# Two exponentials issued behind an output eviction, FFT butterflies behind mixing sums, and an input split into quarters

## The chip, the cores and the metric

The kernel runs on one core of a Trainium2 chip. The metric is the device time of one execution in microseconds (us). Three executions of the kernel before gave 787.26, 787.35 and 787.60 us, and their median, 787.35 us, is the time before.

The core has a matrix engine (TensorE, here PE), a vector engine (DVE), a scalar or activation engine (ACT), a general engine (GpSimd, here POOL) and a queue that issues most transfers (SyncE, here SP). Each engine works through its own list of instructions in order and waits at an instruction until what that instruction reads is there and what it overwrites is done with. SBUF is the on-chip memory, PSUM the accumulators that PE writes.

## What is computed

One encoder layer on x of 2048 rows by 1024 columns, in float32: a projection of all rows, two token mixers, an output projection and a norm.

```python
proj = jnp.einsum('bsd,de->bse', x, w_in[l])
q, k, v, gf_lr, gb_lr, z_gla, u, z_fnet = jnp.split(proj, _OFFSETS, axis=-1)
...
log_af = jax.nn.log_sigmoid(gf_lr @ w_gate_up_fwd + b_gate_fwd) / GATE_TAU
o = _gla_chunked(q, k, v, log_af) + flip(_gla_chunked(flip(q), flip(k), flip(v), flip(log_ab)))
y_gla = rms_norm(o) * gla_norm_g * jax.nn.silu(z_gla)
...
uf = jnp.fft.fft2(ug, axes=(1, 3), norm='ortho').real
y_fnet = einsum(uf, w_fnet) * jax.nn.silu(z_fnet)
...
x = _layernorm(DEEPNORM_ALPHA * x + concatenate([y_gla, y_fnet]) @ w_out, ln_g, ln_b)
```

(The lines are condensed.) The first mixer is a gated linear attention in both directions, four heads; the second is a Fourier transform over the 2048 positions and over the 128 columns of each of four groups.

## The kernel before, in words

Products keep float32 accuracy: `split` (L52) writes an operand as a rounded high part (a cast on ACT, L55) and a low part (a subtraction on DVE, L58), and each product is three matmuls: high by high, high by low, low by high. The rows are taken in eight blocks of 256. There are four stages, one after the other on PE.

**First stage (to about 262 us).** The projections for the two output gates and for u.

**Second stage (262 to 398 us), `phase2`.** Two generators take turns in a loop (L738): `qk_all` (L708), the projections to q and k, and `fnet_pe` (L675), the Fourier branch. `qk_block` (L608) is 96 matmuls of one block at L86, in four runs of 24, and yields after each run. Its x comes through `load_x` (L71): two halves of 128x1024, each a load into `xraw` (two buffers) and one split into `xhl` (four buffers), made at the start of the block before. For each group of 128 columns, `fft(g)` (L515) does the butterflies of a 16-point transform on DVE (L522, L523, L534, L531; `fw` is the array that they work on) and splits the result into four tiles `bhl`. `stage2` (L620) multiplies these with a table (L635) and splits the product into `yhl`; `mixdown` (L640) multiplies that with the group's map (L655) into two PSUM tiles, one of which ACT copies to `qs`, and DVE writes their sum and difference to `yf` (L661, L662). While PE works through the five sets `ks` of one group, DVE also does the butterflies of the next one, a piece at each `next(nf)` (L693, L700). `gate_f` (L665) then multiplies `yf` with the gate on POOL. `et` and `wcs` are the tables, split in the same way.

**Third stage (398 to about 580 us), `phase3`.** The attention, in a loop over b (L963) in which three blocks overlap. PE projects block b to gate inputs and v (`pw_part`, `pv_part`, L94), transposes the gate inputs `rn` (L813; ACT copies the result to `R`, L814) and multiplies them up to gates (L825). For block b-1 it makes scores (L905, L906), and for b-1 and b-2 state updates (L928) and outputs (L935) in `gla_b`. ACT copies a state update to `S` (L930, L932) and the output to `oi` (L939). DVE sums the gates (two scans, L843 and L845), subtracts the value in the chunk's middle (L866) and clips (L867). `gates3` (L869) then takes two exponentials on ACT (L872 into `c`, L873 into `g`), two products on DVE (L891 into `qp`, L892 into `g`), and `alphas`: four small sums on DVE into `tf` and two small exponentials (L952, L953). `chain_f` (L1199) carries the state from chunk to chunk on POOL: an addition (L1194), which needs `S`, and a product with `alpha` (L1197). `gate_evac` (L779) takes a gate input tile from PSUM: two casts on ACT (L781, L782) and a subtraction on DVE (L783), once for each half of the block's rows.

**Fourth stage (to the end), `phase4`.** Output projection (L1220), residual and norm.

The order on each engine is chosen by a scheduler from the order in which the program is written and its estimates of durations. `issue_after(x)` is an extra rule for it: what is written inside comes behind x in the list of x's own engine. It adds no wait. Inside `gates3` it takes hold where x runs on the same engine.

Of the kernel before, what the change touches and what calls it, by code (L numbers as in the profile page):

```python
# [43 lines left out]
class Kern:  # L44
# [454 lines left out]
    def phase2(self):  # L499
        nc, a = self.nc, self.a  # L500
        with ExitStack() as ctx:
# [138 lines left out]
            def mixdown(g, ks, yhl, yv):  # L640
# [11 lines left out]
                for i in (1, 0):  # L652
                    pp = self.pg([P, 2, P])
                    for j, (s, mv) in enumerate(((0, 0), (0, 1), (1, 0))):
# [4 lines left out]
                nc.scalar.copy(out=qs[:, 0:n], in_=pq[0][:, 0:n])  # L659
                k0 = ks[0]  # L660
                nc.vector.tensor_tensor(out=yv[:, k0:k0 + n, :], in0=pq[1][:, 0:n], in1=qs[:, 0:n], op=ALU.add)  # L661
                nc.vector.tensor_tensor(out=yv[:, 16 - k0:16 - k0 - n:-1, ::-1], in0=pq[1][:, 0:n],  # L662
                                        in1=qs[:, 0:n], op=ALU.subtract)

            def gate_f(g, yf):  # L665
                for b in range(NBLK):
                    zf = yps[1].tile([P, BLK], F32, name="zfl", tag="zfl", bufs=4)
                    nc.sync.dma_start(out=zf, in_=self.zf_d[b][:, g, :])
                    yb = yf[:, b * BLK:(b + 1) * BLK]
                    (nc.gpsimd if g < 3 else nc.vector).tensor_tensor(out=yb, in0=yb, in1=zf, op=ALU.mult)  # L670
                    if b % 2:
                        bs = slice((b - 1) * BLK, (b + 1) * BLK)
                        nc.sync.dma_start(out=self.mf_d[:, g, bs], in_=yf[:, bs])

            def fnet_pe():  # L675
                bt = bt0
# [8 lines left out]
                for g in range(4):  # L685
# [4 lines left out]
                    for ks in ((1, 2), (3, 4), (5, 6), (7,), (0, 8)):  # L690
                        with self.tc.issue_after(self.qk_mm.ins):
                            yhl = stage2(g, bt, ks)
                        next(nf, None)  # L693
                        yield
                        if pend:
                            pend()
                        pend = lambda a=(g, ks, yhl, yv): mixdown(*a)
                        if ks[0] == 0:
                            pend = lambda a=(g, ks, yhl, yv), yf=yf: (mixdown(*a), gate_f(a[0], yf))
                        next(nf, None)  # L700
                        yield
# [6 lines left out]
            def qk_all():  # L708
                xn = self.x0
                for b in range(NBLK):  # L710
                    xh = xn
                    if b + 1 < NBLK:
                        xn = self.load_x(b + 1)
                    yield from qk_block(b, xh)

            ga, gb = qk_all(), fnet_pe()
            def wvg_load():
# [33 lines left out]
    def phase3(self):  # L751
# [16 lines left out]
        with ExitStack() as ctx:  # L768
# [194 lines left out]
            for b in range(NBLK):  # L963
# [12 lines left out]
                if b > 1:  # L976
                    with after(self.ks_ev, self.at_ev):
                        gates2(b - 1, prev)
                        gates3(b - 1, prev)
                if b > 2:  # L980
                    self.chain_f(2 * b - 3, 2 * b - 1)
                qk_load(b, blk)
# [413 lines left out]
```

## Time and profile before

| | |
|---|---|
| median of three executions | 787.35 us |
| the profiled execution | 788.25 us |
| its span from first to last instruction | 786.5 us |
| mean granted clock of PE, of full speed | 0.995 |
| busy: PE, DVE, ACT, POOL | 748.6, 549.8, 381.1, 196.5 us |
| PE busy from 262 to 398 us (136 us) | 131.23 us |
| PE busy from 398 to 580 us (182 us) | 169.55 us |

A busy time is the sum over an engine's instructions. A row of the timeline gives start, duration, engine, line of the kernel, operation, tile written and tiles read, and in brackets how long the engine stood idle before it and which instruction ended that. Rows of equal instructions that follow each other are joined (x16). The view of waits adds up such idle times by what ended them.

### The profile page before, as it was taken

To read this page: it belongs to the slowest core of one execution; us is meant where nothing else is said; L and a number is where in the kernel's file an instruction comes from. 1 tells how busy PE (TensorE), PEld (TensorE's weight loads), DVE (VectorE), ACT (ScalarE), POOL (GpSimd) and SP (SyncE) were. 2 spreads that over 40 slices of the span, in tenths; PEclk is the share of its full clock that TensorE was granted. 3 is DMA by queue.
4 is the path that set the end of the run, shared out by engine and by line. 5 is a ranking of instruction groups with operands and counts; after the bars stand their busy time and mean duration, and the time that the engine had idled before them with its cause. 6 is when DMAs were issued, how large, how long until landed. Compare 5 with 4: busy or idle time off the path is not lost.

```text
span 786.5 us, 13529 instructions
## 1 busy us (share of the span) xinstructions
PE 748.6 (95%) x5254; PEld 691.2 (88%) x5254; DVE 549.8 (70%) x808; ACT 381.1 (48%) x707; POOL 196.5 (25%) x137
## 2 busy tenths in 40 slices
PE   6999999999999998989999989999998999999995
PEld 5988899999999998989999888889876788888884
DVE  4693467464545789895748888888868777776764
ACT  6674372233223453445546777776655334334341
POOL 0000003020211000213310414444454454544531
PEclk9999999999999999999999999999999999999998
DMA  8876352444126974555775664555455454444222
GB/s 244 267 210 186 118 192 72 150 114 140 68 94 179 272 239 164 156 168 190 239 214 163 185 184 156 154 166 158 139 175 219 168 184 165 166 144 172 108 81 85
DMA packets 81935, 130.75 MB, mean 166 GB/s; under 512 B 7523, under 2 KB 55651, under 8 KB 81862
## 3 DMA queue, kind: packets, MB, share of 16 engines
q1 hardware_dynamic: 79558, 125.60, 50.5%
q10 hardware_dynamic: 2304, 4.20, 1.5%
q8 instruction: 43, 0.70, 0.4%
q14 instruction: 30, 0.25, 0.1%
HBM read 93.07 MB, written 36.70 MB: 165 GB/s over the span
## 4 chain that ended last, share of the span: by engine, by line
PE 55%; DVE 21%; ACT 11%; DMA 8%; issue 3%; SPq 1%; POOL 0%; DVEq 0%; ACTq 0%
PE mm L1220 17%; PE mm L374 17%; PE mm L86 4%; DMA xraw<-in_xt_dram 3%; DVE c L845 3%; PE mm L291 3%; PE mm L94 2%; DVE c L843 2%; ACT xhl L55 2%; DVE fw L534 2%; PE pa L635 2%; DMA fw<-u_d 2%; DVE fw L531 1%; PE pg L291 1%; PE pa L291 1%
## 5 line engine op out<-in xcount | busy, mean ns | idle before, releaser
L94 PE MATMUL mm<-wA_w,xhl 128*128 128x272 f32 x768 | 105.1, 292 | 0.0
L94 PEld LDWEIGHTS mm<-wA_w,xhl 128*128 128x128 f32 x768 | 98.6, 189 | 0.0
L86 PE MATMUL mm<-xhl,wC_w 128*128 128x256 f32 x768 | 96.0, 284 | 0.0
L86 PEld LDWEIGHTS mm<-xhl,wC_w 128*128 128x128 f32 x768 | 93.7, 192 | 0.5 <-issue 0.5
L1220 PE MATMUL mm<-wA_w,mix 128*128 128x512 f32 (+1 forms) x384 | 90.0, 384 | 1.5 <-ACT mix L55 1.1
L1220 PE MATMUL mm<-wB_w,mix 128*128 128x512 f32 (+1 forms) x384 | 89.3, 387 | 0.0
L1220 PEld LDWEIGHTS mm<-wA_w,mix 128*128 128x128 f32 x384 | 70.3, 188 | 16.6 <-ACT mix L55 1.5
L1194 POOL TENSOR_TENSOR S<-S 64x512 f32<-64x512 f32 x30 | 51.2, 1708 | 124.2 <-ACT S L930 121.2
L1220 PEld LDWEIGHTS mm<-wB_w,mix 128*128 128x128 f32 x384 | 69.5, 189 | 13.0
L58 DVE TENSOR_TENSOR xhl<-xraw,xhl 128x1024 fp32r<-128x1024 f32 (+1 forms) x52 | 57.5, 1111 | 29.8 <-ACT xhl L55 29.5
L55 ACT CAST xhl<-xraw 128x1024 fp32r<-128x1024 f32 (+1 forms) x52 | 49.3, 951 | 39.3 <-DMA xraw<-in_xt_dram 20.0
L55 ACT CAST x<-xraw 128x1024 fp32r<-128x1024 f32 x28 | 29.3, 1048 | 69.0 <-PE mm L374 54.9
L436 POOL TENSOR_TENSOR t<-t,t 128x512 f32<-128x512 f32 x7 | 10.9, 1557 | 190.4 <-ACT t L435 190.4
L1318 POOL TENSOR_TENSOR r<-r,lnb 128x1024 f32<-128x1024 f32 x15 | 35.7, 2383 | 89.5 <-issue 51.2
L58 DVE TENSOR_TENSOR x<-xraw,x 128x1024 fp32r<-128x1024 f32 x28 | 37.8, 1352 | 28.7 <-ACT x L55 28.7
L670 POOL TENSOR_TENSOR yf<-yf,zfl 128x256 f32<-128x256 f32 x24 | 20.9, 900 | 121.3 <-ACT yf L649 111.9
L1197 POOL TENSOR_TENSOR S<-S,alpha 64x512 f32<-64x512 f32 x30 | 48.6, 1620 | 2.4
L374 PE MATMUL mm<-wC_s,x 128*128 128x256 f32 x384 | 48.2, 283 | 0.0
L374 PEld LDWEIGHTS mm<-wC_s,x 128*128 128x128 f32 x384 | 47.1, 192 | 0.1
L291 PE MATMUL mm<-xhl,wA_w 128*128 128x512 f32 x192 | 43.9, 389 | 0.0
L291 PEld LDWEIGHTS mm<-xhl,wA_w 128*128 128x128 f32 x192 | 36.0, 188 | 7.4
L55 ACT CAST mix<-zg 128x512 fp32r<-128x512 f32 x15 | 9.3, 622 | 58.8 <-POOL zg L1289 56.0
(210 smaller groups left out, 1497.3 us busy)
## 6 DMA issues: line engine op xcount, KB each, us to landing
xraw<-in_xt_dram SPq DMA_DIRECT2D x48, 512.0 KB, 4.7
xr<-in_x_dram SPq DMA_DIRECT2D x16, 512.0 KB, 3.6
out_dram<-r SPq DMA_DIRECT2D x15, 512.0 KB, 2.7
xraw<-in_xt_dram SPq DMA_DIRECT2D x24, 256.0 KB, 4.7
zg_d<-zs SPq DMA_DIRECT2D x32, 128.0 KB, 3.7
u_d<-t SPq DMA_DIRECT2D x16, 256.0 KB, 3.2
zf_d<-t SPq DMA_DIRECT2D x16, 256.0 KB, 2.4
zfl<-zf_d SPq DMA_DIRECT2D x32, 128.0 KB, 3.4
```

The costliest lines, as they stand in the source:

```text
L55: nc.scalar.copy(out=hi, in_=src)
L58: return (lo_eng or nc.vector).tensor_tensor(out=lo, in0=src, in1=f32(hi), op=ALU.subtract)
L86: mm = self.nc.tensor.matmul(ps, w[:, s, k, c0:c0 + P], x[:, m, k % 4, :], start=(k == 0 and i == 0), stop=(k == KB - 1 and i == 2))
L94: self.nc.tensor.matmul(ps, x[:, s, k % 4, t * P:(t + 1) * P], w[:, m, k, c0:c0 + cols], start=(k == 0 and i == 0), stop=(k == KB - 1 and ...
L291: nc.tensor.matmul(ps[c], self.wzg[:, s, 2 * q + kk, c * P:(c + 1) * P], x[:, m, kk], start=(q == 0 and kk == 0 and j == 0), stop=(q == 3 ...
L374: nc.tensor.matmul(ps[:, i], s_[s][:, k, i * P:(i + 1) * P], m_[m][:, k], start=(k == 0 and j == 0), stop=(k == 3 and j == 2))
L670: (nc.gpsimd if g < 3 else nc.vector).tensor_tensor(out=yb, in0=yb, in1=zf, op=ALU.mult)
L845: V.tensor_tensor_scan(out=c2[64:128, ::-1], data0=r2[64:128, ::-1], data1=g2[64:128, ::-1], initial=0.0, op0=ALU.mult, op1=ALU.add)
L1194: E.tensor_tensor(out=S[ds, dst], in0=S[ds, dst], in1=S[ds, src], op=ALU.add)
L1197: E.tensor_tensor(out=d3, in0=d3, in1=al, op=ALU.mult)
L1220: nc.tensor.matmul(y, c["mix"][:, s, eb], w[:, v, eb % 4, lo:lo + m], start=(ebs[0] == 4 and i == 0), stop=(ebs[0] == 0 and i == len(seq) ...
L1318: nc.gpsimd.tensor_tensor(out=r, in0=r, in1=lnb, op=ALU.add)
```

## The change

Three edits. The two exponentials of `gates3`, from b=2 on, are also to come behind the last copy into `oi` (L939) on ACT. The first butterfly piece of each set of `ks` is to come behind the last difference into `yf` (L662) on DVE. And x for blocks 1 to 7 of the q and k projections is split in quarters: both halves are still loaded at the start of the block before, but a quarter (128x512) is split after each of that block's four yields.

```diff
--- before.py
+++ after.py
@@ -659,7 +659,7 @@
                 nc.scalar.copy(out=qs[:, 0:n], in_=pq[0][:, 0:n])
                 k0 = ks[0]
                 nc.vector.tensor_tensor(out=yv[:, k0:k0 + n, :], in0=pq[1][:, 0:n], in1=qs[:, 0:n], op=ALU.add)
-                nc.vector.tensor_tensor(out=yv[:, 16 - k0:16 - k0 - n:-1, ::-1], in0=pq[1][:, 0:n],
+                self.mix_ev = nc.vector.tensor_tensor(out=yv[:, 16 - k0:16 - k0 - n:-1, ::-1], in0=pq[1][:, 0:n],
                                         in1=qs[:, 0:n], op=ALU.subtract)
 
             def gate_f(g, yf):
@@ -671,6 +671,8 @@
                     if b % 2:
                         bs = slice((b - 1) * BLK, (b + 1) * BLK)
                         nc.sync.dma_start(out=self.mf_d[:, g, bs], in_=yf[:, bs])
+
+            self.mix_ev = None
 
             def fnet_pe():
                 bt = bt0
@@ -690,7 +692,11 @@
                     for ks in ((1, 2), (3, 4), (5, 6), (7,), (0, 8)):
                         with self.tc.issue_after(self.qk_mm.ins):
                             yhl = stage2(g, bt, ks)
-                        next(nf, None)
+                        if self.mix_ev is None:
+                            next(nf, None)
+                        else:
+                            with self.tc.issue_after(self.mix_ev.ins):
+                                next(nf, None)
                         yield
                         if pend:
                             pend()
@@ -708,10 +714,19 @@
             def qk_all():
                 xn = self.x0
                 for b in range(NBLK):
-                    xh = xn
-                    if b + 1 < NBLK:
-                        xn = self.load_x(b + 1)
-                    yield from qk_block(b, xh)
+                    xh, xn, raws = xn, [], []
+                    for hf in range(2 if b + 1 < NBLK else 0):
+                        raw = self.xpool.tile([P, 4, BLK], F32, name="xraw", tag="xraw", bufs=2)
+                        nc.sync.dma_start(out=raw, in_=a["xt"][b + 1, :, 4 * hf:4 * hf + 4, :])
+                        raws.append(raw)
+                    for i, _ in enumerate(qk_block(b, xh)):
+                        yield
+                        if raws and i < 4:
+                            if i % 2 == 0:
+                                t = self.xpool.tile([P, 2, 4, BLK], F32R, name="xhl", tag="xhl", bufs=4)
+                                xn.append(t)
+                            t, js = xn[-1], slice(i % 2 * 2, i % 2 * 2 + 2)
+                            self.split(t[:, 0, js], t[:, 1, js], raws[i // 2][:, js])
 
             ga, gb = qk_all(), fnet_pe()
             def wvg_load():
@@ -976,7 +991,8 @@
                 if b > 1:
                     with after(self.ks_ev, self.at_ev):
                         gates2(b - 1, prev)
-                        gates3(b - 1, prev)
+                        with after(self.oi_ev):
+                            gates3(b - 1, prev)
                 if b > 2:
                     self.chain_f(2 * b - 3, 2 * b - 1)
                 qk_load(b, blk)
```

The lists of PE and POOL are the same as before. Those of ACT and DVE each have 14 splits of 128x1024 replaced by 28 of 128x512. Three places in the lists follow. In the changed kernel line numbers are higher: by 15 in most of `phase2`'s end and `phase3`.

ACT, one turn of the third stage (b=4), before: from the first exponential (L872) to the second half's gate input (`rn`):

```order
L872 ACTIVATE c<-g 128x1024
L781 CAST rn<-mm 128x32
L782 CAST rn<-mm 128x32
L873 ACTIVATE g<-g 128x1024
L930 COPY S<-pg 64x512
L797 COPY v<-mm 128x240
L932 COPY S<-pg 64x512
L939 COPY oi<-pg 128x512
L952 ACTIVATE alpha<-tf 64x8
L953 ACTIVATE alpha<-tf 64x8
L781 CAST rn<-mm 128x32
L782 CAST rn<-mm 128x32
```

and with the change (L887 and L888 are the exponentials, L945 and L947 the copies into `S`, L954 the one into `oi`, L967 and L968 those into `alpha`):

```order
L796 CAST rn<-mm 128x32
L797 CAST rn<-mm 128x32
L812 COPY v<-mm 128x240
L945 COPY S<-pg 64x512
L947 COPY S<-pg 64x512
L954 COPY oi<-pg 128x512
L887 ACTIVATE c<-g 128x1024
L967 ACTIVATE alpha<-tf 64x8
L968 ACTIVATE alpha<-tf 64x8
L888 ACTIVATE g<-g 128x1024
L796 CAST rn<-mm 128x32
L797 CAST rn<-mm 128x32
```

Both exponentials now stand behind the three copies, and the first half's gate input and v ahead of them.

DVE, the start of the second stage, before: x of qk block 1 is the `xhl` row of 128x1024 here and one further ahead:

```order
L534 TENSOR_TENSOR fw<-fw 128x384
L58 TENSOR_TENSOR xhl<-xraw,xhl 128x1024
L534 TENSOR_TENSOR fw<-fw 128x384
L531 SCALAR_TENSOR_TENSOR fw<-fw 128x128 x16
L58 TENSOR_TENSOR et<-eraw,et 128x384
L58 TENSOR_TENSOR bhl<-fw,bhl 128x512 x4
L58 TENSOR_TENSOR et<-eraw,et 128x384
L58 TENSOR_TENSOR xhl<-xraw,xhl 128x1024
```

and with the change:

```order
L531 SCALAR_TENSOR_TENSOR fw<-fw 128x128 x8
L58 TENSOR_TENSOR xhl<-xraw,xhl 128x512
L531 SCALAR_TENSOR_TENSOR fw<-fw 128x128 x8
L58 TENSOR_TENSOR xhl<-xraw,xhl 128x512
L58 TENSOR_TENSOR bhl<-fw,bhl 128x512 x4
L58 TENSOR_TENSOR xhl<-xraw,xhl 128x512
```

The second half of block 1's x was split ahead of the last 16 products and of `bhl`; now two quarters stand among and behind these products, and the last quarter behind all four `bhl`.

DVE, the second stage's group 0, before (L531 are butterflies of the group after next):

```order
L58 TENSOR_TENSOR yhl<-pa,yhl 128x512
L58 TENSOR_TENSOR bhl<-fw,bhl 128x512
L531 SCALAR_TENSOR_TENSOR fw<-fw 128x128 x9
L661 TENSOR_TENSOR yf<-pg,qs 128x2x128
L662 TENSOR_TENSOR yf<-pg,qs 128x2x128
L531 SCALAR_TENSOR_TENSOR fw<-fw 128x128 x6
L58 TENSOR_TENSOR bhl<-fw,bhl 128x512
```

and with the change:

```order
L58 TENSOR_TENSOR yhl<-pa,yhl 128x512
L58 TENSOR_TENSOR bhl<-fw,bhl 128x512
L661 TENSOR_TENSOR yf<-pg,qs 128x2x128
L662 TENSOR_TENSOR yf<-pg,qs 128x2x128
L58 TENSOR_TENSOR bhl<-fw,bhl 128x512
L58 TENSOR_TENSOR yhl<-pa,yhl 128x512
```

The butterflies between the rows of this group's sums are gone; they follow after the group's fourth set.

## Rows read from the trace of the kernel before

**Rows 1.** The page, part 1: busy us, share of the span, instructions
```profile
PE 748.6 (95%) x5254; PEld 691.2 (88%) x5254; DVE 549.8 (70%) x808; ACT 381.1 (48%) x707; POOL 196.5 (25%) x137
```

**Rows 2.** The view of waits, PE: us in total, times, longest us
```profile
PE mm L813 <- DVE rn L783: 5.1, 6, 1.0
PE pg L655 <- DVE yf L662: 4.0, 4, 1.6
PE mm L825 <- ACT R L814: 2.7, 5, 0.8
```

**Rows 3.** Timeline, PE, second stage: start us, us, line, tiles, [idle before <-releaser]
```profile
307.16 0.86 PE L655 MATMUL pg<-yhl,wcs 128*128 128x256 f32 x5 [0.78 <-DVE yhl L58]
...
314.26 0.62 PE L655 MATMUL pg<-yhl,wcs 128*128 128x256 f32 x3 [1.56 <-DVE yf L662]
...
391.46 0.55 PE L655 MATMUL pg<-yhl,wcs 128*128 128x128 f32 x3 [0.30 <-DVE yf L662]
```

**Rows 4.** Timeline, DVE, ahead of the stall at 314.26
```profile
311.37 1.91 DVE L531 SCALAR_TENSOR_TENSOR fw<-fw 128x128 f32<-128x128 f32 x9
...
313.61 0.59 DVE L662 TENSOR_TENSOR yf<-pg,qs 128x256 f32<-128x256 f32 x1
```

**Rows 5.** Timeline, PE, the first two qk blocks
```profile
262.50 16.76 PE L86 MATMUL mm<-xhl,wC_w 128*128 128x256 f32 x135
```

**Rows 6.** Timeline, DVE, while these blocks run
```profile
271.58 1.23 DVE L58 TENSOR_TENSOR xhl<-xraw,xhl 128x1024 fp32r<-128x1024 f32 x1 [0.93 <-ACT xhl L55]
...
273.19 3.32 DVE L531 SCALAR_TENSOR_TENSOR fw<-fw 128x128 f32<-128x128 f32 x16
276.42 0.56 DVE L58 TENSOR_TENSOR et<-eraw,et 128x384 fp32r<-128x384 f32 x1
276.88 2.50 DVE L58 TENSOR_TENSOR bhl<-fw,bhl 128x512 fp32r<-128x512 f32 x4
```

**Rows 7.** Timeline, PE, third stage, one turn of the loop (b=4)
```profile
466.08 0.73 PE L825 MATMUL mm<-R,wg 98*128 98x256 f32 x4 [0.50 <-ACT R L814]
...
478.72 1.06 PE L935 MATMUL pg<-at,v 128*128 128x128 f32 x8
479.53 4.75 PE L94 MATMUL mm<-wA_w,xhl 128*128 128x272 f32 x36
...
485.36 0.32 PE L813 MATMUL mm<-ident,rn 128*96 128x128 f32 x1 [0.97 <-DVE rn L783]
...
487.68 0.51 PE L825 MATMUL mm<-R,wg 98*128 98x256 f32 x2 [0.49 <-ACT R L814]
```

**Rows 8.** Timeline, ACT, the same turn
```profile
480.37 1.06 ACT L872 ACTIVATE c<-g 128x1024 f32<-128x1024 f32 x1 [2.48 <-DVE g L867]
...
483.88 0.59 ACT L939 COPY oi<-pg 128x512 f32<-128x512 f32 x1
...
484.81 0.19 ACT L781 CAST rn<-mm 128x32 fp32r<-128x32 f32 x1
```

**Rows 9.** Timeline, DVE, the same turn, and a later clip twice
```profile
479.58 0.69 DVE L867 TENSOR_SCALAR g<-g 128x1024 f32<-128x1024 f32 x1
...
482.71 1.22 DVE L892 TENSOR_TENSOR g<-kr,g 128x1024 f32<-128x1024 f32 x1
...
564.79 0.42 DVE L867 TENSOR_SCALAR g<-g 128x512 f32<-128x512 f32 x1
...
569.31 1.38 DVE L867 TENSOR_SCALAR g<-g 128x512 f32<-128x512 f32 x1
```

**Rows 10.** Timeline, POOL, the same turn, and two later adds
```profile
483.15 1.90 POOL L1194 TENSOR_TENSOR S<-S 64x512 f32<-64x512 f32 x1 [5.43 <-ACT S L930]
485.13 1.03 POOL L1197 TENSOR_TENSOR S<-S,alpha 64x512 f32<-64x512 f32 x1
...
568.62 1.78 POOL L1194 TENSOR_TENSOR S<-S 64x512 f32<-64x512 f32 x1 [4.91 <-ACT S L930]
...
583.61 1.27 POOL L1194 TENSOR_TENSOR S<-S 64x512 f32<-64x512 f32 x1 [1.93 <-ACT S L932]
```

## Prediction

> **What bounds the kernel.** I read the page's busy times first. PE is busy for 748.6 of 786.5 us [rows 1], so an edit pays only as far as it shortens PE's list or takes one of its gaps away. The change leaves PE's list as it is. All it can do is move the moment at which PE's data are ready, so the second view is that of PE's waits. Three entries belong to what is moved: the transposes of the gate inputs wait for DVE's `rn` (5.1 us), the mixing matmuls for DVE's sums into `yf` (4.0 us), the gate matmuls for ACT's copy to `R` (2.7 us) [rows 2]. Third, the timelines around these gaps, for who is late and why.
>
> In the second stage the reader should see that DVE is late with short work because long work stands ahead of it. PE waits 1.56 us at 314.26 [rows 3]; the difference into `yf` that it needs starts at 313.61, behind nine butterflies for a later group, 1.91 us [rows 4]. In the third stage a turn takes 21.60 us, from the gate matmuls at 466.08 to those at 487.68, with waits of 0.97 us for `rn` and 0.49 us for `R` [rows 7]. `rn` is late because ACT's cast comes only at 484.81, behind both exponentials and three copies [rows 8].
>
> **Butterflies behind the mixing sums: -4.5 us.** The gaps for `yf` are four, together 4.0 us; the last, 0.30 us [rows 3], lies in the last group, where there are no butterflies, and stays. The 0.78 us at 307.16 for `yhl` [rows 3] has the same cause: butterflies and a whole half of x stand ahead. That makes 4.0 - 0.30 + 0.78 = 4.5 us that can go, and no instruction is added. The butterflies take the same DVE time, later; what then becomes late is the split into `bhl` of the next group, and behind it `yhl`. I charge 0.5 us for that in groups 1 and 2, since some of the four gaps may return in a smaller form. The bounds of this charge are nothing and all of the gaps that are not in group 0, what is left beside 0.78 and 1.56: 4.5 - 0.8 - 1.6 = 2.1 us.
>
> **x in quarters: +1.5 us.** The splits cost DVE and ACT about the same time in all. A quarter behind each yield relieves `yhl` and the sums (counted above) but has a price at the start. Block 1's last quarter stands behind the four `bhl` splits. In the profile 135 matmuls of the q and k projections take 16.76 us, 0.124 us each, from 262.50 [rows 5]; block 0 is 96 of them and ends at 274.4, and block 1 reads the last quarter at its 19th matmul, at 274.4 + 18 x 0.124 = 276.6. DVE ends `bhl` at 276.88 + 2.50 = 279.4 [rows 6]. With the change what stands ahead is less by the idle 0.93 us at 271.58, one table split (0.46 us, the step from 276.42 to 276.88) and one quarter (half of 1.23) [rows 6], so it ends at about 277.4. The quarter adds 0.6, and PE has its data at 278.0 to 278.1: a new wait of about 1.5 us. Its bounds are 0 (DVE runs a little further ahead than I reckon) and 3 (the idle time comes back, with the quarters' casts waiting for their load, and the split lands at 279.4 + 0.6 less half a microsecond). For the later blocks I take nothing: there the last quarter has a whole run of 24 matmuls, 3.0 us by the same 0.124, as cover. If that cover goes, each block start can cost as much as this one (the third rival).
>
> Second stage: -4.5 + 0.5 + 1.5 = **-2.5 us** (from -4.5 to -4.5 + 2.1 + 3 = +0.6).
>
> **Exponentials behind the `oi` copy: -2.2 us.** PE ends the output matmuls that `oi` is copied from at about 479.8 (478.72 + 1.06) [rows 7], but ACT copies only at 483.88 [rows 8]. Put first, the copy can end by about 480.5 and the first exponential start there, against 480.37 before [rows 8]: it loses next to nothing. Two exponentials of 1.06 and two short ones of 0.2 end by 483.1, and `rn` is cast at 483.2 instead of 484.81. On DVE the product L892 (1.22 us) [rows 9] still stands ahead of the subtraction into `rn`; it would end at about 484.3 and the transposes run at 484.5 instead of 485.36 [rows 7]. That alone takes the wait for `rn`, and with it the one for `R`: five turns (b=3 to 7) at 0.98 and four (b=3 to 6) at 0.49 are 6.9 us, the upper bound.
>
> I do not take it, because of POOL. The chain's addition starts right behind the copies into `S`, at 483.15 now [rows 10], and would start at about 479.6. What happens when it meets DVE is in the rows. Alone the addition takes 1.27 us (583.61); started while DVE ran L892 (482.71 to 483.93) [rows 9], it took 1.90 us [rows 10]. And a clip of 128x512 that takes 0.42 us by itself took 1.38 us at 569.31 [rows 9], while POOL's addition ran from 568.62 to 570.40 [rows 10]: whichever comes second stands still until the first is done. At 479.58 DVE starts the clip [rows 9], 0.02 us ahead of POOL by my reckoning. If the clip is first, the addition runs from 480.2 to about 481.5, the sums into `tf` follow, `alpha` is there at about 482.2, and POOL's product with it (1.03 us [rows 10]) comes between L891 (to 482.9) and L892, which then runs from 483.95 to about 485.1. So `rn` is subtracted at 485.2 and the transposes gain perhaps 0.2 us; the wait for `R` goes (0.49 us), since ACT's next splits are already done. That is about 0.7 us in each of the turns 4, 5 and 6, 2.1 us, and 0.1 us in turn 7. In turn 3 the addition comes before the clip, and I take nothing. The bounds are 0 and -6.9; I stay near 0 because a row for each collision stands there.
>
> The Trainium skill's page "SBUF — State Buffer", section "Who interferes with whom", says that DVE and GpSimd share a port pair as an exclusive lock that whoever issues first holds for the whole instruction, but that a DVE instruction with at most one SBUF input, outside the two-port modes, does not contend. The trace agrees with the lock (1.90 against 1.27 us). By the clause on one input the clip would never be held up: turn 3 would gain its 0.7 us too, this part would be -2.9, and rival 2 could not occur. The stalled clip, which has one SBUF input (1.38 against 0.42 us), speaks against reading it so, unless the clip runs in a two-port mode.
>
> **Sum.** -2.5 - 2.2 = -4.7 us. Against the profiled execution's own 788.25 us (its span is 786.5 us) that is 783.55; the median of the three executions is 0.9 us lower than that execution, and 787.35 - 4.7 = 782.65 us is what I forecast.
>
> **Rivals.**
>
> 1. *No collision.* The chain's addition fits between DVE's instructions, and the full 6.9 us of the third stage go: 787.35 - 2.5 - 6.9 = 778.0 us. For it: nothing but the order of a few tenths of a microsecond decides. Against: the rows on POOL and the clip.
>
> 2. *The collision takes it all.* POOL's addition comes ahead of the clip in every turn (0.02 us decides), the first exponential starts 1.2 us later, and the third stage gives nothing: 787.35 - 2.5 = 784.9 us. If moreover half of the second stage's gain returns as waits for `bhl`, 786.5 us. For it: turn 3.
>
> 3. *Slower: late quarters.* At the starts of the qk blocks the last quarter is late in all of blocks 1 to 7, as I reckon it for block 1, because DVE, which is already behind with the butterflies, reaches it only after `yhl` and `bhl`. Seven such waits of 1.5 us are 10.5; with the 4.5 gained and 2.2 from the third stage that gives 787.35 + 10.5 - 4.5 - 2.2 = 791.2 us. It decides from about five late blocks. For it: the scheduler puts three quarters in a row ahead of group 0's first `yhl`, which shows that they are emitted late. Against: only block 1's last quarter has both sixteen products and all four `bhl` (3.32 + 2.50 us [rows 6]) ahead of it.
>
> 4. *No change.* The new rules are about order alone; if what they move was hidden, nothing happens. The lists show that they take hold (the butterflies are gone from between the sums), so this needs the gaps to come back elsewhere in full: 787.35 us.
>
> **How the numbers follow.** My forecast has 0.50, rival 1 0.15, rival 2 0.17, rival 3 0.09 and rival 4 0.09. Two tenths of a per cent, 1.6 us, is about what a measurement can tell from no change. The forecast and rival 1 are faster by more, and so is most of rival 2 (0.12): 0.77. Within 0.2% lie the rest of rival 2 (0.05), rival 4 (0.09) and a trace of rival 3: 0.15. Slower is 0.08. The range reaches from rival 1's 778.0 to 787.2, which takes in rival 2 and the bounds of the second stage, and leaves out rival 3, half of rival 4 and what lies beyond rival 1.
>
> **What would show it.** Right: the wait of the mixing matmuls for `yf` falls from 4.0 to below 1 us; a new wait at L86 for `xhl` of 1 to 2 us near 277; the wait for `R` all but gone, the one for `rn` still about 4 us; POOL's addition in a steady turn 3 to 4 us earlier than now and longer than 1.27 us; and a turn of about 20.9 us. Wrong: a turn of 20.2 us (rival 1) or of 21.6 us with DVE's clip stretched to over 1.5 us (rival 2), or waits at L86 in more than one block (rival 3).

## The result, and the profile after

The changed kernel takes 799.25 us (median of 4 executions, 796.38 to 799.34), the kernel before 787.48 us (4 executions): the ratio is 1.0124, 95% interval 1.0098 to 1.0151. It is slower; 782.65 us was forecast. The profiled execution took 799.27 us and its span is 797.5 us, 11.0 more than before.

The view of PE's waits, with the three entries of [rows 2] and a new one (us in total, times, longest us):

```profile
PE mm L828 <- DVE rn L798: 14.7, 6, 3.0
...
PE pg L655 <- DVE yf L662: 1.4, 2, 1.2
...
PE mm L86 <- DVE xhl L58: 1.2, 1, 1.2
...
PE mm L840 <- ACT R L829: 0.8, 1, 0.8
```

The wait for `yf` has shrunk, to 1.4 us where below 1 was forecast, and the one at L86 is there as forecast. But the wait for `rn`, which was to stay near 4 us, is 14.7 us. Where the 11.0 us come from is read off the first gate matmul of each turn (L825 before, L840 now):

| stretch | before, us | after, us | difference |
|---|---|---|---|
| start to the first matmul of qk block 0 | 262.50 | 262.90 | +0.4 |
| second stage, from there to the first gate matmul (407.62, now 405.39) | 145.12 | 142.49 | -2.6 |
| to the gate matmuls of b=2 (442.36, now 440.16) | 34.74 | 34.77 | 0.0 |
| the turn to b=3 | 23.72 | 25.11 | +1.4 |
| the turns to b=4, 5 and 6 | 21.60, 21.59, 21.59 | 24.05, 24.02, 23.95 | +7.2 |
| the turn to b=7 (551.83, now 561.20) | 20.97 | 23.91 | +2.9 |
| from there to the end | 234.7 | 236.3 | +1.6 |

So the second stage gained what was forecast (-2.5), and the loss is in the five turns in which the exponentials were moved, 11.6 us. The first row and the last lie outside the edits and were not followed; the last stretch takes 231.5 to 236.5 us in the traces of the runs below, 231.5 in e7, which edits nothing in it. One of the five turns on PE, to be laid beside [rows 7]:

```profile
502.69 4.75 PE L94 MATMUL mm<-wA_w,xhl 128*128 128x272 f32 x36
...
510.43 0.45 PE L828 MATMUL mm<-ident,rn 128*96 128x128 f32 x1 [2.88 <-DVE rn L798]
510.53 2.97 PE L94 MATMUL mm<-wA_w,xhl 128*128 128x272 f32 x12
513.34 0.64 PE L840 MATMUL mm<-R,wg 98*128 98x256 f32 x4
```

PE is through with its matmuls at the same distance as before, then stands still for 2.88 us instead of 0.97. And the twelve matmuls after that, which took 1.75 us before (485.44 to 487.19), take 2.8. ACT, with the list that the section on the change shows ([rows 8] before):

```profile
501.18 0.19 ACT L796 CAST rn<-mm 128x32 fp32r<-128x32 f32 x1 [0.26 <-PE mm L94]
...
503.90 0.36 ACT L812 COPY v<-mm 128x240 f32<-128x240 f32 x1 [2.44 <-DVE rn L798]
504.15 0.58 ACT L945 COPY S<-pg 64x512 f32<-64x512 f32 x1
...
505.36 0.59 ACT L954 COPY oi<-pg 128x512 f32<-128x512 f32 x1
505.98 1.06 ACT L887 ACTIVATE c<-g 128x1024 f32<-128x1024 f32 x1
...
507.39 1.06 ACT L888 ACTIVATE g<-g 128x1024 f32<-128x1024 f32 x1
508.35 0.17 ACT L796 CAST rn<-mm 128x32 fp32r<-128x32 f32 x1
```

and DVE ([rows 9]):

```profile
501.38 1.20 DVE L881 TENSOR_TENSOR g<-c 128x1024 f32<-128x1024 f32 x1
...
502.62 0.69 DVE L882 TENSOR_SCALAR g<-g 128x1024 f32<-128x1024 f32 x1
...
503.67 0.19 DVE L798 TENSOR_TENSOR rn<-mm,rn 128x32 fp32r<-128x32 f32 x1
507.07 1.22 DVE L906 TENSOR_TENSOR qp<-qp,c 128x1024 f32<-128x1024 f32 x1 [3.21 <-ACT c L887]
508.48 1.79 DVE L907 TENSOR_TENSOR g<-kr,g 128x1024 f32<-128x1024 f32 x1 [0.19 <-DMA oi_d<-oi]
510.20 0.18 DVE L798 TENSOR_TENSOR rn<-mm,rn 128x32 fp32r<-128x32 f32 x1
```

The row to look at is ACT's copy of v at 503.90: it waits 2.44 us, and what releases it is DVE's subtraction into `rn` at 503.67. DVE comes to that only behind the subtraction of the middle, the clip and the sums into `tf`. Behind the copy of v, in ACT's own list, wait the copies into `S`, the copy into `oi`, and both exponentials. The first exponential now starts 16.66 us after the turn's first gate matmul (505.98 - 489.32); before it was 14.29 (480.37 - 466.08). That is 2.4 us later, while the forecast had it 0.1 later.

From there the lateness reaches PE by way of DVE. ACT's cast for the second half of `rn` comes 19.03 us into the turn (508.35), against 18.73 before (484.81 in [rows 8]), only 0.3 us later: from the end of its wait of 2.4 us to that cast ACT needs 4.45 us, as before (4.44), with its work in another order. But the exponentials now stand at the end of that work. DVE's product L907 needs the second one (507.39 to 508.45), and the subtraction into `rn` stands behind L907 in DVE's list, so it runs only at 510.20, when the cast has long been there. Before, DVE was done with both products and waited for the cast.

POOL, beside [rows 10]:

```profile
504.88 1.28 POOL L1210 TENSOR_TENSOR S<-S 64x512 f32<-64x512 f32 x1 [4.11 <-ACT S L945]
507.28 1.91 POOL L1213 TENSOR_TENSOR S<-S,alpha 64x512 f32<-64x512 f32 x1 [1.12 <-ACT alpha L967]
```

The addition does not meet the clip at all (502.62 to 503.31), but the product with `alpha` stands in front of L907, which needs 1.79 us instead of 1.22.

The clock of the matmuls after the wait is in the view of stretches (length, then PE, PEld, DVE, ACT and POOL busy, all in us, then PEclk, the granted clock as a share of full speed, and last what the DMA engines did):

```profile
463.60:465.20 1.60, 1.60 (x13) 1.60 (x14) 1.60 (x2) 0.71 (x3) 0.00 (x0) 1.00 0.15 20
486.35:489.30 2.95, 2.95 (x13) 2.95 (x14) 2.95 (x4) 0.71 (x3) 0.00 (x0) 0.50 0.49 139
510.45:513.30 2.85, 2.85 (x13) 2.85 (x14) 2.85 (x4) 0.69 (x3) 0.00 (x0) 0.51 0.51 131
...
505.00:507.50 2.50, 2.50 (x21) 2.29 (x19) 0.43 (x1) 2.40 (x6) 1.38 (x2) 1.00 0.29 116
```

Up to the wait PE had the full clock, 2.4 GHz (505 to 507.5); after 2.88 us of standing still it worked at the lower level, 1.2 GHz, for the twelve matmuls. After the first such wait, 3.05 us to 463.60, it did not fall. The twelve matmuls cost 1.05 us more at the lower clock, in four of the five turns.

That accounts for the loss: five waits for `rn` of 3.05, 2.88, 2.88, 2.86 and 2.83 us in place of 4.9 in all is +9.6; four waits for `R` gone, -2.0; four times 1.05 of clock, +4.2; together 11.8, against 11.6 read from the table.

### The profile page after: what moved, and what is told of

Its sections match the earlier page's. It is cut to its first block, busy times and chain, and to the rows that moved or that the text cites. A ratio compares the mean times of both kernels' runs of the same rounds, so it can differ in the third digit from the quotient of the medians.

```text
span 797.5 us, 13547 instructions
## 1 busy us (share of the span) xinstructions
PE 753.7 (95%) x5254; PEld 697.8 (87%) x5254; DVE 554.8 (70%) x822; ACT 384.2 (48%) x721; POOL 200.4 (25%) x137
## 4 chain that ended last, share of the span: by engine, by line
PE 63%; DVE 17%; ACT 9%; DMA 7%; issue 3%; SPq 1%; POOL 0%; DVEq 0%; ACTq 0%
PE mm L374 18%; PE mm L1236 18%; PE mm L86 8%; PE mm L291 5%; DVE c L860 3%; PE mm L94 3%; PE pa L635 2%; DVE c L858 2%; DMA xraw<-in_xt_dram 1%; DMA zg<-zg_d 1%; PE pg L291 1%; PE pa L291 1%; PE mm L231 1%; DMA oi_d<-oi 1%; DVE g L853 1%
## 5 line engine op out<-in xcount | busy, mean ns | idle before, releaser
L94 PE MATMUL mm<-wA_w,xhl 128*128 128x272 f32 x768 | 110.0, 300 | 0.0
L94 PEld LDWEIGHTS mm<-wA_w,xhl 128*128 128x128 f32 x768 | 103.5, 198 | 0.0
L86 PE MATMUL mm<-xhl,wC_w 128*128 128x256 f32 x768 | 96.3, 284 | 1.2 <-DVE xhl L58 1.2
L86 PEld LDWEIGHTS mm<-xhl,wC_w 128*128 128x128 f32 x768 | 93.8, 192 | 1.9 <-DVE xhl L58 1.5
L1236 PE MATMUL mm<-wA_w,mix 128*128 128x512 f32 (+1 forms) x384 | 92.2, 391 | 1.8 <-ACT mix L55 1.8
L1236 PEld LDWEIGHTS mm<-wA_w,mix 128*128 128x128 f32 x384 | 72.2, 193 | 17.0 <-ACT mix L55 2.1
L58 DVE TENSOR_TENSOR xhl<-xraw,xhl 128x1024 fp32r<-128x1024 f32 (+2 forms) x66 | 58.4, 901 | 32.4 <-ACT xhl L55 28.4
L1210 POOL TENSOR_TENSOR S<-S 64x512 f32<-64x512 f32 x30 | 47.3, 1578 | 129.4 <-ACT S L945 126.7
L55 ACT CAST xhl<-xraw 128x1024 fp32r<-128x1024 f32 (+2 forms) x66 | 50.7, 791 | 48.1 <-DMA xraw<-in_xt_dram 28.4
L436 POOL TENSOR_TENSOR t<-t,t 128x512 f32<-128x512 f32 x7 | 10.9, 1558 | 190.8 <-DVE t L428 122.9
L1213 POOL TENSOR_TENSOR S<-S,alpha 64x512 f32<-64x512 f32 x30 | 53.4, 1779 | 7.6 <-ACT alpha L967 5.6
L670 POOL TENSOR_TENSOR yf<-yf,zfl 128x256 f32<-128x256 f32 x24 | 23.9, 1024 | 116.3 <-ACT yf L649 106.7
```

The lines of the kernel that those rows point to most:

```text
L55: nc.scalar.copy(out=hi, in_=src)
L58: return (lo_eng or nc.vector).tensor_tensor(out=lo, in0=src, in1=f32(hi), op=ALU.subtract)
L86: mm = self.nc.tensor.matmul(ps, w[:, s, k, c0:c0 + P], x[:, m, k % 4, :], start=(k == 0 and i == 0), stop=(k == KB - 1 and i == 2))
L94: self.nc.tensor.matmul(ps, x[:, s, k % 4, t * P:(t + 1) * P], w[:, m, k, c0:c0 + cols], start=(k == 0 and i == 0), stop=(k == KB - 1 and ...
L1210: E.tensor_tensor(out=S[ds, dst], in0=S[ds, dst], in1=S[ds, src], op=ALU.add)
L1213: E.tensor_tensor(out=d3, in0=d3, in1=al, op=ALU.mult)
```

## The experiments

Three theories were put up. **A, the queue:** the pin (the new rule that the exponentials come behind the copy into `oi`) puts the exponentials behind a copy that waits for DVE. **B, the lock:** POOL's product ahead of L907 makes `rn` late. **C:** the second stage's edits cost. The kernels before took between 785 and 795 us on the chips of these runs, so each kernel is compared by its ratio to the runs of before on its own chip. "Turn" is from the gate matmuls of b=4 to those of b=5, with the waits for `rn` and `R` in it.

| kernel | us, median | ratio (95%) | turn | rn, R |
|---|---|---|---|---|
| before | 787.48 | 1 | 21.59 | 0.98, 0.49 |
| changed | 799.25 | 1.0124 (1.0098 to 1.0151) | 24.02 | 2.88, 0 |
| e1 no pin | 786.76 | 0.9976 (0.9957 to 0.9996) | 21.58 | 0.96, 0.48 |
| e2 pin only | 803.18 | 1.0178 (1.0143 to 1.0212) | 24.27 | 2.72, 0 |
| e3 v first | 782.68 | 0.9930 (0.9905 to 0.9955) | 20.68 | 0.81, 0 |
| e4 alpha late | 793.75 | 1.0069 (1.0051 to 1.0087) | 22.74 | 1.89, 0 |
| e5 v first, alpha late | 783.74 | 0.9927 (0.9899 to 0.9954) | 20.94 | 0.68, 0 |
| e6 butterflies only | 785.01 | 0.9951 (0.9931 to 0.9970) | 21.60 | as before |
| e7 quarters only | 788.98 | 0.9999 (0.9977 to 1.0021) | 21.58 | as before |
| e8 e5, block 1 in halves | 780.35 | 0.9898 (0.9868 to 0.9929) | 20.95 | as e5 |
| e9 no pin, rn first | 783.93 | 0.9922 (0.9901 to 0.9944) | 21.59 | 0, 1.06 |
| e10 pin, swap, alpha early | 777.42 | 0.9863 (0.9843 to 0.9883) | 20.51 | 0.66, 0 |
| e11 e8 with the swap | 773.44 | 0.9797 (0.9778 to 0.9816) | 20.31 | 0, 0 |
| e13 e11 without the pin | 784.14 | 0.9946 (0.9928 to 0.9964) | 21.84 | 1.56, 0 |

### One edit taken away, and one alone

e1 is the changed kernel without this:

```diff
-                        with after(self.oi_ev):
-                            gates3(b - 1, prev)
+                        gates3(b - 1, prev)
```

> The change without its first edit: the exponentials are not pinned, butterflies and quarters stay. Theory A (queue): the pin alone costs, because on ACT the copies into S and oi stand behind the copy of v, v waits for DVE's subtraction into rn, and DVE does that only behind the clip and the sums into tf; the exponentials so start 2.4 us later in a turn. Then this kernel keeps the second stage's gain of about 2.5 us and has the turns of before (21.6 us, wait for rn about 1.0): about 785 us, ratio 0.997. Theory B (lock): POOL's product ahead of the product L907 is what makes rn late; then the same here, since the pin made them meet. Theory C (the second stage's edits cost, and the third stage only follows): slower than before, 795 us or more.

e2 is the kernel before with that edit alone.

> The kernel before with the pin as its only edit. Theories A and B: all of the loss and none of the second stage's gain, about 802 us, ratio 1.018, turns of 24.0 us. Theory C: no slower than before.

Both came out as A and B have it, and C falls: without the pin the turns are back at 21.6 us and the second stage's gain stands (786.76 us, ratio 0.9976); the pin alone costs 1.8%, 13.0 us of it in the five turns.

### Queue or lock

e3 leaves the pin and takes the waiting copy out of its way. The copy of v is written between the casts of `rn` and DVE's subtraction:

```diff
                 self.rn_ev = nc.scalar.copy(out=rn[:, t, 64:96].bitcast(F32R), in_=sl)
+                if v is not None:
+                    nc.scalar.copy(out=v[:, 272:512], in_=pg_[:, 0:240])
                 V.tensor_tensor(out=rn[:, t, 32:64].bitcast(F32R), in0=sl, in1=rn[:, t, 0:32], op=ALU.subtract)
```

> The changed kernel with the copy of v written ahead of DVE's subtraction into rn, so that ACT's copy of v no longer waits for DVE. Theory A: the chain v, S, oi, exponentials runs as early as I had first reckoned, and the pin pays as forecast: turns of 20.3 to 20.9 us (21.6 if POOL's addition always beats the clip), wait for rn 0.2 to 0.8 us, 779 to 783 us, ratio 0.989 to 0.994. Theory B: the collision with POOL remains in force (additions come earlier still), so turns stay above 22 us, 790 us or more.

Measured: 782.68 us, turns of 20.68 us. ACT in such a turn, then DVE and PE:

```profile
495.61 0.38 ACT L799 COPY v<-mm 128x240 f32<-128x240 f32 x1
...
497.55 0.59 ACT L955 COPY oi<-pg 128x512 f32<-128x512 f32 x1
498.16 1.06 ACT L888 ACTIVATE c<-g 128x1024 f32<-128x1024 f32 x1
```

```profile
496.89 0.69 DVE L883 TENSOR_SCALAR g<-g 128x1024 f32<-128x1024 f32 x1
497.50 1.26 DVE L963 TENSOR_TENSOR cst<-cst,cmid 128x8 f32<-128x8 f32 x1
...
500.67 1.79 DVE L908 TENSOR_TENSOR g<-kr,g 128x1024 f32<-128x1024 f32 x1 [0.19 <-DMA oi_d<-oi]
```

```profile
502.62 0.32 PE L829 MATMUL mm<-ident,rn 128*96 128x128 f32 x1 [0.81 <-DVE rn L800]
```

The copy of v has no wait, the first exponential starts at 498.16, 14.55 us into the turn (gate matmuls at 483.61), and the order of events is the one that the prediction had reckoned with: the clip just ahead of POOL's addition (497.06), a sum held up behind it (1.26 us at 497.50), POOL's product ahead of L908 (1.79 us), and 0.8 us of waiting for `rn` left. In the turn to b=3 the addition comes before the clip, also as reckoned. So A holds: it was one waiting copy in ACT's queue that cost the loss. The five turns take 106.2 us here, 121.0 in the changed kernel and 109.5 before.

The addition takes 1.67 us when it starts during the clip, against 1.28 by itself (504.88 above). So the clip, though it reads one array, holds POOL's addition up too, as the prediction took from the stalled clip of [rows 9].

e4 leaves v where it was and takes POOL's product out of DVE's way instead:

```diff
-                nc.scalar.activation(out=alpha[0:64, lo:n1], in_=tf[0:64, 0:m], func=AF.Exp, scale=1.0 / TAU)
-                nc.scalar.activation(out=alpha[64:128, lo + 1:n1 + 1], in_=tf[64:128, 0:m], func=AF.Exp, scale=1.0 / TAU)
+                with after(*evs):
+                    nc.scalar.activation(out=alpha[0:64, lo:n1], in_=tf[0:64, 0:m], func=AF.Exp, scale=1.0 / TAU)
+                    nc.scalar.activation(out=alpha[64:128, lo + 1:n1 + 1], in_=tf[64:128, 0:m], func=AF.Exp, scale=1.0 / TAU)
```

with `self.rn_ev` of the second half as the event.

> The changed kernel with the two small exponentials into alpha issued behind the second half's rn casts, so that POOL's product with alpha can no longer stand ahead of DVE's product L907. Theory B: rn is in time, the wait falls to 1 us or less and the turn to 21.6 us or less, about 785 us. Theory A: only the lock's share goes (0.57 us of L907's hold-up and 0.45 us of ACT's time ahead of the second exponential): the wait for rn falls from 2.9 to about 1.9 us; the turn to 23 us if PE's clock still falls afterwards and to about 22 us if it does not: 788 to 795 us.

Measured: 793.75 us, waits for `rn` of 1.9 to 2.2 us, turns to b=4 to 6 of 22.7 to 23.2 us. B as the main cause falls; POOL's product has a share of 0.7 to 1.0 us of the 2.9, with alpha's own 0.45 us on ACT in it, as A had it.

### What is left of the lock

e5 has both edits.

> v copied first and alpha's exponentials late, both on the changed kernel. Theory A (queue), with the lock as a second, smaller price: with v copied first the turn was 20.68 us with 0.80 us of waiting for rn left; that rest is the lock's (POOL's product ahead of L907), so it goes: turns of about 20.1 us, wait for rn 0.3 us or less, about 2.4 us less than with v first alone, 780 to 781 us, ratio 0.990. A rival for the rest: ACT is simply full between the oi copy and the rn casts; then the 0.80 us stay and the time is that of v first alone, 782.7 us.

This missed: turns of 20.94 us, not 20.1, and no gain over e3. The product no longer meets L908, but here the addition came first:

```profile
497.53 1.44 POOL L1212 TENSOR_TENSOR S<-S 64x512 f32<-64x512 f32 x1 [1.53 <-ACT S L946]
```

```profile
496.63 1.21 DVE L882 TENSOR_TENSOR g<-c 128x1024 f32<-128x1024 f32 x1
497.75 1.25 DVE L963 TENSOR_TENSOR cend<-cend,cmid 128x8 f32<-128x8 f32 x1
498.92 0.68 DVE L883 TENSOR_SCALAR g<-g 128x1024 f32<-128x1024 f32 x1
```

```profile
498.04 0.59 ACT L955 COPY oi<-pg 128x512 f32<-128x512 f32 x1
499.69 1.06 ACT L888 ACTIVATE c<-g 128x1024 f32<-128x1024 f32 x1 [1.07 <-DVE cst L963]
```

POOL's addition gets in at the end of the subtraction of the middle; the small sum behind that (0.16 us by itself) is held up to 1.25 us, the clip starts at 498.92, and the exponential waits 1.07 us for it. This is the collision of the prediction's rival 2, but not its whole loss: the turn is 0.65 us shorter than before. It came about because alpha's exponentials now stand ahead of ACT's casts of x, which puts DVE's splits of x (they wait 0.44 us for ACT at 503.69) and all that follows later: the subtraction of the middle starts 12.6 us into the turn (496.63 - 484.03), in e3 12.0 (495.64 - 483.61), while POOL's addition starts 13.5 us into it in both.

e11 settles the race by the order of two copies, on top of e8 (below):

```diff
-                if n + 1 < NCH:
-                    nc.scalar.copy(out=S[0:64, n + 1], in_=up[0:64])
                 if n > 0:
-                    nc.scalar.copy(out=S[64:128, n - 1], in_=up[64:128])
+                    sb = nc.scalar.copy(out=S[64:128, n - 1], in_=up[64:128])
+                with (after(sb) if n > 0 else after()):
+                    if n + 1 < NCH:
+                        nc.scalar.copy(out=S[0:64, n + 1], in_=up[0:64])
```

> Block 1 in halves, v first and alpha late, with the two copies into S in the other order, so that POOL's addition starts 0.6 us later. In the kernel with v first and alpha late the first exponential waited 1.07 us because POOL's addition came ahead of DVE's sums and clip. If that race is what is left, the clip now runs first: exponential right behind the oi copy, wait for rn 0.3 us, turns of 20.4 to 20.6 us instead of 20.95, 778.5 to 779.5 us. If not, 780.4 us as with block 1 in halves.

Measured: 773.44 us, ratio 0.9797: better than expected, and faster than both kernels. In all five turns the clip now starts ahead of the addition, so the first exponential no longer waits for it. A collision is still there (the small sum behind the clip takes 1.27 us), but it stands behind what the exponential needs. PE has no wait left for `rn` or `R` in these turns:

```profile
492.44 0.59 ACT L958 COPY oi<-pg 128x512 f32<-128x512 f32 x1
493.06 1.06 ACT L890 ACTIVATE c<-g 128x1024 f32<-128x1024 f32 x1
...
495.45 0.19 ACT L798 CAST rn<-mm 128x32 fp32r<-128x32 f32 x1 [0.25 <-PE mm L94]
```

```profile
492.27 0.69 DVE L885 TENSOR_SCALAR g<-g 128x1024 f32<-128x1024 f32 x1
492.88 1.27 DVE L966 TENSOR_TENSOR cst<-cst,cmid 128x8 f32<-128x8 f32 x1
```

```profile
492.49 1.63 POOL L1215 TENSOR_TENSOR S<-S 64x512 f32<-64x512 f32 x1 [2.09 <-ACT S L951]
```

```profile
496.77 0.60 PE L831 MATMUL mm<-ident,rn 128*96 128x128 f32 x2
...
498.73 0.66 PE L843 MATMUL mm<-R,wg 98*128 98x256 f32 x4
```

Of the 7.3 us between the spans of e8 (778.8) and e11 (771.5) 4.6 lie in the turns to b=3 to 7 (106.74 and 102.18 us); 1.15 is a wait for `yf` in the second stage that is in e8's trace and not in e11's, and the rest, outside both, was not followed. That wait is not the swap's: e10 and e13 below have the swap and the same second stage, and have the wait.

e10 is e11 with alpha's exponentials where the changed kernel has them.

> The kernel with the swapped copies, with the pin, but alpha's exponentials left ahead of the second big one as in the changed kernel. POOL's product then meets DVE's products again. By the lock: the product L907 is held up by about 0.6 us, rn waits 0.5 to 0.8 us, turns of 20.6 to 20.9 us, 775 to 777 us. If the swap alone removed the collisions: 773.5 us.

Measured: 777.42 us, turns of 20.51 us, `rn` waits 0.66 us, L910 (the same product) takes 1.79 us. The lock's wait is then 0.66 us a turn, as expected, but the turn is only 0.20 us longer than e11's: there the output matmuls, right behind DVE's `at`, start 12.85 us into the turn, here 12.51. The turn and the time just miss the 20.6 to 20.9 us and the 775 to 777 us that were expected. Of the 3.8 us between the spans of e10 and e11 (775.3 and 771.5) 1.8 lie in the five turns and 2.3 ahead of the first gate matmul, where the two kernels are written the same.

e13 is e11 without the pin.

> The kernel with the swapped copies, without the pin: v first, alpha late, copies into S in the other order, block 1 in halves all stay. It asks what the pin itself is worth. If ACT's order was only ever harmful through the wait of v, and the other edits do the rest: turns of 20.3 us again, 773 to 774 us. If the second exponential must come after the copies for the lock to be avoided: turns of 20.9 to 21.6 us, 776 to 780 us.

Measured: 784.14 us, turns of 21.84 us, slower than both expectations. On ACT:

```profile
497.11 1.06 ACT L890 ACTIVATE c<-g 128x1024 f32<-128x1024 f32 x1 [2.48 <-DVE cst L966]
498.07 0.17 ACT L798 CAST rn<-mm 128x32 fp32r<-128x32 f32 x1
...
500.17 1.06 ACT L891 ACTIVATE g<-g 128x1024 f32<-128x1024 f32 x1
501.13 0.17 ACT L798 CAST rn<-mm 128x32 fp32r<-128x32 f32 x1
```

```profile
502.64 0.32 PE L831 MATMUL mm<-ident,rn 128*96 128x128 f32 x1 [1.56 <-DVE rn L802]
```

Without the pin the scheduler puts the first exponential ahead of the casts and copies that are ready; ACT stands idle for 2.48 us until the clip is done, and the copies and the second exponential come after that: the second half's cast of `rn` comes 18.66 us into the turn (501.13 - 482.47), in e11 17.03 (495.45 - 478.42). So the pin is worth 7.7 us in the five turns (109.9 and 102.2 us), once no copy ahead of it waits for DVE. The spans differ by 10.9 us (782.4 and 771.5, on two chips); the rest is 1.0 us ahead of the first gate matmul, the wait for `yf` above for the most part, and 2.2 behind the turns, not followed.

### The same aim without the pin

e9 moves the other side: the backward copy into `S` and the one into `oi` are written behind the second half's casts of `rn`, from b=3 on, and the pin is gone. Block 1's x is in halves, as in e8 below; v and alpha are as in the changed kernel. The lines that place the copies (the edit has more, which only make it possible to write them there):

```diff
                 pw_part(xh, 1, blk, range(4, KB))
+                if b > 2:
+                    with after(self.rn_ev):
+                        late[0]()
```

> No pin; instead the second half's rn casts come ahead of two copies that nobody waits for (the backward half of the copies into S, and oi), in turns 3 to 7; butterflies behind the sums and quarters from block 2 on stay. If rn was late only because ACT's casts stood behind copies that can wait, PE's waits for rn and for R both fall below 0.3 us a turn: turns of 20.2 to 20.5 us, 778 to 779.5 us, ratio 0.987. If DVE's product L892, held up by POOL's addition, is what ends last: wait for rn 0.8 us, turn 20.9 us, 781 to 782 us.

This missed as well. The wait for `rn` is gone, but the turn is 21.59 us as before:

```profile
480.98 0.19 ACT L799 CAST rn<-mm 128x32 fp32r<-128x32 f32 x1
...
482.05 0.59 ACT L957 COPY oi<-pg 128x512 f32<-128x512 f32 x1
482.67 1.99 ACT L55 CAST xhl<-xraw 128x1024 fp32r<-128x1024 f32 x2
484.56 0.36 ACT L831 CAST R<-mm 96x256 fp32r<-96x256 f32 x1
```

```profile
484.98 0.74 PE L842 MATMUL mm<-R,wg 98*128 98x256 f32 x4 [1.05 <-ACT R L831]
```

The copies now stand ahead of the two casts of x and of the copy to `R`, and PE waits 1.05 us for `R`. The work on ACT was the same and one exponential still waited for the clip (2.48 us idle); the wait only changed its name.

### The second stage

e6 and e7 have the second and the third edit alone on the kernel before.

> The kernel before with the butterflies' rule as its only edit. If the gaps for yf are the whole gain of the second stage: -3 to -4 us there, the wait of the mixing matmuls for yf down from 4.0 to about 1 us, no wait at L86, and 784 us in all, ratio 0.9955. If the quarters are needed as well (whole halves of x still stand ahead of the sums): half of that, 786 us.

> The kernel before with the quarters as its only edit. By my reckoning they cost at block 1 (a wait at L86 of 1.2 to 1.5 us) and save the 0.8 us at yhl: about 788 us, ratio 1.001. If quarters are what frees DVE: faster than before by 1 us or more.

The butterflies alone give 0.5% (785.01 us), the quarters nothing (788.98 us, ratio 0.9999): the times are those of the first expectation of each. The details are not: in e6 one wait for `yf` of 2.23 us is left and one of 0.30, where about 1 us was expected, and its trace has the second stage only 1.6 us shorter; with the quarters the longer wait is 1.15 us. In e7 the wait at L86 is 0.74 us. e8 has e5's edits and splits block 1's x in halves again:

```diff
+                    if b == 0:
+                        xn = self.load_x(1)
-                    for hf in range(2 if b + 1 < NBLK else 0):
+                    for hf in range(2 if 0 < b < NBLK - 1 else 0):
```

> v first, alpha late, and block 1's x still split in halves as before (quarters from block 2 on). If the wait at L86 is the price of putting block 1's last quarter behind bhl, it goes and with it 1.2 us: 779 us, ratio 0.9885. If the wait only moves (bhl later, and the first yhl with it): the time of v first with alpha late alone.

Measured: 780.35 us against 783.74 on the same chip. The 288 matmuls of the first three blocks run in one row without a wait:

```profile
263.35 35.12 PE L86 MATMUL mm<-xhl,wC_w 128*128 128x256 f32 x288
```

That the wait at block 1 was the price of the quarter behind `bhl` is shown by its absence. The 3.4 us are more than the 1.3 us of that wait; the remainder was not followed, and is within what the executions of e5 and e8 spread (781.08 to 784.77 and 779.75 to 782.64).

## Why the prediction was wrong

**Right, second stage.** The sum was -2.5 us, measured -2.6 in the trace, and e1 as a whole gave a ratio of 0.9976, some 1.9 us. One trace of this stage is good to about 1 us: in e2, which edits nothing there, it reads 1.1 us longer than before. By terms: the gaps that were to go (4.5 us) left 1.15 us behind in one place, where 0.5 was charged; the wait at block 1 was forecast at 1.5 us and is 1.25, at 278.50 where 278.0 to 278.1 was reckoned. Later blocks have no wait at L86, as forecast, so rival 3, the slower one, did not happen.

**Wrong: "Put first, the copy can end by about 480.5".** The step took the `oi` copy to be bound only by PE's output matmuls. In ACT's list with the change, which the section on the change shows, the copy of v stands ahead of the copies into `S` and `oi`, and the sum has no term for it. It waits for DVE's subtraction into `rn` (2.44 us), which stands behind the clip on DVE. In the profile before this wait could not be seen, since the first exponential, which needs the clip, stood ahead of v in the same queue and took the wait on itself. With the pin the exponential came to stand behind v, so the same 2.4 us of waiting for the clip, which had stood ahead of the first exponential [rows 8], now stood ahead of v and the three copies, and both exponentials came behind them. The first exponential starts 16.66 us into the turn; 14.4 was forecast (480.5 - 466.08), and e3, without the wait, has 14.55. The times behind it in the forecast's chain (483.1 to 485.2) moved with it: `rn` is late because L907 is, which stands ahead of its subtraction on DVE, as the prediction had the order.

**Right in mechanism, in another place: the lock.** The prediction's picture of the turn, with 0.7 us gained and 0.8 us of `rn` left, is e3, where v does not wait: 20.68 us a turn (20.9 forecast), 0.9 gained and 0.80 left, 3.3 us in the five turns where 2.2 was forecast. That the time of e3, 782.68 us, is the forecast for the change to 0.03 us is luck: on its chip the kernel before took 788.45 us, and the ratio is 0.9930 where the forecast's was 0.9940. The addition ahead of the sums and the clip, rival 2, did not happen in the changed kernel and did in e5, where it took only a part of the gain. Rival 1's gain, the waits for `rn` and `R` gone, came in e11, but not for rival 1's reason: the collision is there and PE does not wait for it. One sum of the rivals does not come out: with half of the second stage's 2.5 us returned rival 2 is at 786.1 us, not 786.5; nothing hangs on it.

**Not on the list: PE's clock.** The forecast had no term for it. A wait of 2.9 us was followed by twelve matmuls at half the clock in four of five turns, 4.2 us in all, more than a third of the loss.

**The range.** Its upper end, 787.2, came from the same picture. The only slower rival was in the other stage; a mechanism on the side of the exponentials, a new wait in ACT's queue, was not among them, and the range was too narrow for leaving it out.

## What to carry to other kernels

Before an instruction is pinned behind another, list every instruction that comes to stand ahead of it in that queue and ask for each what it waits for, its wait on other engines included; a wait that does not show in the old trace can be hidden by the very instruction that is moved. Here one copy, written ahead of one subtraction instead of behind it, turned a loss of 1.2% into a gain of 0.7%, and three further changes (alpha's exponentials later, block 1 in halves, two copies swapped) made it 2.0%. Where two engines hold each other up, look at the order of arrival: taking one collision away alone (e5) only moved another one into place, and swapping two copies of 0.6 us took its wait off the exponential.

## What was not expected of the hardware and the program

Two engines that only read the same PSUM tile were ordered: the copy of v waits for DVE's subtraction into `rn` when it is written behind it, and does not when it is written ahead (e3). The runs show the wait, not why it is put there. A reason stands in the Trainium skill, page "PSUM — Partial Sum Buffer", section "PSUM bank collisions raise a hardware error": two engines may not access one bank in the same partitions at once, two reads included, so software has to order them. Both instructions read the one tile `pw`, of 272 float32 a partition, in the same partitions. The trace agrees as far as it goes: the two never overlap in it (503.67 to 503.86, then 503.90). By that rule it could have been foreseen from the code that one of the two waits; that it is the one written second is what e3 shows. The prediction did not weigh it.

PE's clock fell to 1.2 GHz after waits of 2.88 us and not after one of 3.05 us (e2 shows 0.72 as the mean over the matmuls after a wait of 2.73 us). In e4 it fell after a shorter one: 0.50 after a wait of 2.15 us (554.25), while after one of 2.20 us (462.78) it stayed at 1.00. So in these runs the length of the wait alone does not tell whether the clock falls. After waits of about 1 us, as before, the twelve matmuls took 1.75 us, the full level's time.
